# HGRN of a decoder trunk: log k moved into the exponent of the levels, and level scores summed by three wide additions

## The chip, the cores and the metric

One core of one Trainium2 chip runs the whole program. The metric is the device time of one execution in microseconds (us); lower is better. The kernel before has a median of 681.6 us over 3 runs.

## What is computed

Two residual layers over 512 tokens of width 1024. Each layer normalizes its input, projects it once, runs three mixers, gates them and projects back. The change lies in the second (odd) layer's HGRN mixer: 4 heads of width 64, chunked linear recurrence. With log decay `lf` per token and channel, `b` its running sum inside a chunk, and k = exp(lf - f) for the forget input f:

```
scores = einsum('bhtd,bhsd,bhtsd->bhts', qt, kt, exp(b_t - b_s))   # s <= t
intra  = einsum('bhts,bhse->bhte', scores, vt)
st     = st * exp(b_last) + einsum('bhsd,bhse->bhde', kt * exp(b_last - b), vt)
```

Every factor k appears beside an exponential of a difference of `b`.

## The kernel before, in words

Channels lie on the 128 partitions, the 512 tokens along the row. The 4 heads are worked as two pairs (`hgrn_pair`, called twice from line 1373), each with 128 channels and chunks of 128 tokens. The running sum `b` is one scan (L1147).

A chunk's triangle of scores is built by levels. `level(hh)` cuts the tokens into blocks of 2*hh, takes the last `b` of the first half as reference, and makes one tile `hx`: second half exp(b - ref) times q (L1162, L1164, L1167), first half exp(ref - b) times k (L1163, L1164, L1168). Matmuls of `hx` with itself then give that level's scores. Levels 64 and 32 go straight into the score tiles `hat` (L1179, L1192). Levels 16, 8, 4, 2 (`small`, L1209) and the last two (diagonal and neighbour, `last`, L1218, which uses k itself) are multiplied by masks into six planes of `htm` (L1200), one tile for each head of the pair. L1226 sums the six planes with one strided reduction for each head into `hsm`, and four copies put the result into the diagonal blocks of `hat` (L1228, recorded as L490 on ScalarE or L492 on VectorE). `hat` feeds the matmuls L1255.

For the carried state, `he` = exp(b_last - b) (L1230, L1231) times k (L1232) is transposed by TensorE (L1235) and multiplied with the values (L1245). L1267 to L1273 normalize and gate the output.

Around it stand the input projections of the layer (L235 under `pj`), with weights split into a rounded part `hi` on ScalarE (L226) and a rest `lo` on VectorE (L227). TensorE, VectorE and ScalarE each run their queue in order. The order itself is made when the program is built, by a list planner that takes ready instructions by priority and its own cost estimates. Four bands set the priorities: the straight text (HGRN among it) counts from 0, evacuations of projections from 50, weight splits from 500000, head norms from 600000, projections from 1000000. So projections fill what HGRN leaves on TensorE, and any changed duration can sort the queues anew.

Of the kernel before, what the change touches and what calls it, by code (L numbers as in the profile page):

```python
# [13 lines left out]
AF = mybir.ActivationFunctionType  # L14
OP = mybir.AluOpType
AX = mybir.AxisListType
PSUM = bass.MemoryType.PSUM

P = 128
D = 1024  # L20
S = 512
NM = 256
NT = S // P
# [123 lines left out]
def tile_trunk(ctx, tc, x_in, memT_in, w_mem, e_w_in, e_w_out, o_w_in, o_w_out, ln_g, w2_in, a2_in,  # L147
               prm_in, cst_in, out):
    nc = tc.nc
    V, A, G, T = nc.vector, nc.scalar, nc.gpsimd, nc.tensor  # L150
# [6 lines left out]
    def tl(pool, shape, name, dt=F32, **kw):  # L157
        return pool.tile(shape, dt, tag=name, name=name, **kw)
# [3 lines left out]
    def pj(name="pj"):  # L162
        if name == "t":
            tn[0] ^= 1
            name = f"t{tn[0]}"
        return ps.tile([P, 512], F32, tag=name, name=name, bufs=2 if name == "pj" else 1)
# [22 lines left out]
    def C(name, j=None):  # L189
        return cst[name] if j is None else cst[name][:, j:j + 1]  # L190
# [89 lines left out]
    def col(name, n=1):  # L280
        c = sum(w for _, w in cols.values())
        cols[name] = (c, n)
        return small[:, c:c + n]
# [203 lines left out]
    def evac(dst, src, kind="d"):  # L487
        evac_n[kind] += 1
        if EVP[kind][evac_n[kind] % len(EVP[kind])] == "A":
            A.activation(dst, src, AF.Copy)  # L490
        else:
            V.tensor_copy(dst, src)  # L492
# [169 lines left out]
    with ExitStack() as ph:  # L662
# [10 lines left out]
        for h in range(2):  # L673
            t = pj("t")
# [46 lines left out]
    for n, sgn in (("aq", -0.125), ("ak", 1.0), ("cq", -0.125), ("ck", 1.0)):  # L721
        g = col("g" + n)
        tmp = col("t" + n)
# [409 lines left out]
    def hgrn_pair(dp, q, qx, fd, idn, sgd, rm128):  # L1133
        qd = qx[:, 0]
        f3 = lambda t: t.rearrange("p (c t) -> p c t", t=P)
        e = tl(dp, [P, S], "he")
        lf = tl(dp, [P, S], "hlf")
# [2 lines left out]
        A.activation(e, e, AF.Exp, scale=-1.0)  # L1140
        A.activation(e, e, AF.Ln, bias=ones)
        V.tensor_tensor(lf, lf, e, op=OP.subtract)
        k = tl(dp, [P, S], "hk")
        V.tensor_tensor(k, lf, fd, op=OP.subtract)
        A.activation(k, k, AF.Exp)
        b = tl(dp, [P, S], "hb")
        V.tensor_tensor_scan(b, rm128, lf, 0.0, op0=OP.mult, op1=OP.add)  # L1147
        hs = [slice(0, 64), slice(64, 128)]
        q4 = [slice(32 * j, 32 * j + 32) for j in range(4)]
        at = [tl(dp, [P, NT, P], f"hat{p}", bufs=1) for p in range(2)]  # L1150
        for p in range(2):
            G.memset(at[p], 0.0)
        tmp = [tl(dp, [P, 6, NT, 32], f"htm{p}", bufs=1) for p in range(2)]
        hl = C("hlev").rearrange("p (l t) -> p l t", t=32)

        def level(hh):
            x = tl(dp, [P, S], "hx", bufs=3)
            bv = b.rearrange("p (c z h) -> p c z h", z=2, h=hh)
            xv = x.rearrange("p (c z h) -> p c z h", z=2, h=hh)
            nb = S // (2 * hh)  # L1160
            ref = bv[:, :, 0, hh - 1:hh].to_broadcast([P, nb, hh])
            V.tensor_tensor(xv[:, :, 1, :], bv[:, :, 1, :], ref, op=OP.subtract)  # L1162
            V.tensor_tensor(xv[:, :, 0, :], ref, bv[:, :, 0, :], op=OP.subtract)  # L1163
            A.activation(x, x, AF.Exp)  # L1164
            qv = qd.rearrange("p (c z h) -> p c z h", z=2, h=hh)
            kv = k.rearrange("p (c z h) -> p c z h", z=2, h=hh)
            V.tensor_tensor(xv[:, :, 1, :], xv[:, :, 1, :], qv[:, :, 1, :], op=OP.mult)  # L1167
            V.tensor_tensor(xv[:, :, 0, :], xv[:, :, 0, :], kv[:, :, 0, :], op=OP.mult)  # L1168
            return x

        def lev64():
            x = level(64)
            s = s2()
            for p in range(2):
                for i in range(NT):
                    T.matmul(s[0:64, p, i * 64:i * 64 + 64], x[hs[p], i * P:i * P + 64],
                             x[hs[p], i * P + 64:(i + 1) * P], start=True, stop=True)
            for p in range(2):
                A.activation(at[p][0:64, :, 64:128], s[0:64, p, 0:256].rearrange("p (i t) -> p i t", t=64), AF.Copy)  # L1179

        def lev32():
            x = level(32)
            s = s2()
            for p in range(2):
                for i in range(NT):
                    for m in range(2):
                        o = i * P + 64 * m
                        T.matmul(s[q4[2 * m], p, i * 32:i * 32 + 32], x[hs[p], o:o + 32], x[hs[p], o + 32:o + 64],
                                 start=True, stop=True)
            for p in range(2):  # L1190
                for m in range(2):
                    A.activation(at[p][q4[2 * m], :, 64 * m + 32:64 * m + 64],  # L1192
                                 s[q4[2 * m], p, 0:128].rearrange("p (i t) -> p i t", t=32), AF.Copy)
# [3 lines left out]

        def masked(s, g0):
            for p in range(2):
                V.tensor_tensor(tmp[p][:, g0:g0 + 2], s[:, p, 0:2 * P].rearrange("p (l i t) -> p l i t", l=2, t=32),  # L1200
                                hl[:, g0:g0 + 2, None, :].to_broadcast([P, 2, NT, 32]), op=OP.mult)

        def small(g0):
            s = s2()
            for l in range(2):
                x = level(16 >> (g0 + l))
                for p, i, j, o in blocks:
                    c = l * P + i * 32
                    T.matmul(s[q4[j], p, c:c + 32], x[hs[p], o], x[hs[p], o], start=True, stop=True)  # L1209
            masked(s, g0)  # L1210

        def last():
            s = s2()
            A.activation(qx[:, 1], lf, AF.Exp)
            V.tensor_tensor(qx[:, 1], qx[:, 1], qd, op=OP.mult)
            sv = s[:, :, 0:2 * P].rearrange("p a (l t) -> p a l t", t=P)
            for p, i, j, o in blocks:
                T.matmul(sv[q4[j], p, :, i * 32:i * 32 + 32], k[hs[p], o], qx[hs[p], :, o], start=True, stop=True)  # L1218
            masked(s, 4)

        todo = {"A": lev64, "B": lev32, "0": lambda: small(0), "2": lambda: small(2), "4": last}
        for c in HGO:
            todo[c]()
        for p in range(2):
            sm = tl(dp, [P, NT, 32], "hsm")
            V.tensor_reduce(sm, tmp[p].rearrange("p l i t -> p i t l"), axis=AX.X, op=OP.add)  # L1226
            for j in range(4):
                evac(at[p][q4[j], :, 32 * j:32 * j + 32], sm[q4[j]], "h")  # L1228
        e = tl(dp, [P, S], "he")
        V.tensor_tensor(f3(e), f3(b)[:, :, P - 1:P].to_broadcast([P, NT, P]), f3(b), op=OP.subtract)  # L1230
        A.activation(e, e, AF.Exp)  # L1231
        V.tensor_tensor(e, e, k, op=OP.mult)  # L1232
        t = pj("t")
        for i in range(NT):
            T.transpose(t[:, i * P:(i + 1) * P], e[:, i * P:(i + 1) * P], ident)  # L1235
# [34 lines left out]
        t = pj("t")  # L1270
# [61 lines left out]
    def odd_layer():  # L1332
# [6 lines left out]
        with ExitStack() as ph2:  # L1339
# [32 lines left out]
            for q in range(2):  # L1372
                hgrn_pair(dp, q, qd[q], fd[q], idn, sg[4 + q], rm128)
# [67 lines left out]
```

## Time and profile before

| what | value |
|---|---|
| median of 3 runs | 681.6 us (679.17, 681.6, 681.83) |
| profiled execution, its own time | 678.45 us |
| its span, first to last instruction | 676.2 us |
| mean granted TensorE clock | 0.997 |
| busy share: TensorE / VectorE / ScalarE | 96% / 73% / 49% |
| HGRN stage, from the first scan to the last `hat` matmul | 395 to 455 us of the span |

A busy share is an average over all stages. TensorE's busy time is modelled, so 96% busy does not say that it computes at its peak. The granted clock is given as a share of 2.4 GHz; 0.5 is the lower level, 1.2 GHz. "issue" as a releaser means that the engine waited for nothing that the profile shows.

### The profile page before, as it was taken

The page shows a single profiled execution, that of the slowest core. Times are in us where ns is not written, and L with a number is a line of the kernel's source. Part 1 is how long each engine was busy: PE and PEld are TensorE (multiplying, and loading weights), DVE is VectorE, ACT ScalarE, POOL GpSimd, SP SyncE. Part 2 cuts the span into 40 slices and gives each one's busy share as a digit, 9 for nine tenths or more (in the row PEclk, how much of TensorE's full clock was granted, in tenths as well). Part 3 has the DMA queues.
Part 4 walks back from the last instruction along what each step waited for, and adds up shares of the span by engine and source line. Part 5 has one row for each costly group of instructions (what it writes and reads, how often), then busy time and mean ns, then how long its engine had stood idle before and what let it go on. Part 6 is the DMA issues. An engine that isn't in the chain of part 4 may idle for free.

```text
span 676.2 us, 15423 instructions
## 1 busy us (share of the span) xinstructions
PE 651.4 (96%) x6192; PEld 551.8 (82%) x6192; DVE 491.7 (73%) x1394; ACT 328.2 (49%) x969; POOL 6.8 (1%) x21
## 2 busy tenths in 40 slices
PE   8999999999999998999999999999999999999997
PEld 5877777898888875567999987779999977577997
DVE  4996685888847978857747986985645658789853
ACT  5667346442222357545415585545355336478420
POOL 1000000000000000000000000000000000000000
PEclk9999999999999999999999999899999999999999
DMA  9471222322101340101524433014232331000323
GB/s 303 125 192 31 64 63 64 99 64 64 39 28 38 88 155 5 39 1 40 172 94 126 131 93 96 3 54 127 72 101 89 95 93 32 1 1 0 96 63 124
DMA packets 62905, 53.52 MB, mean 79 GB/s; under 512 B 3377, under 2 KB 61041, under 8 KB 62834
## 3 DMA queue, kind: packets, MB, share of 16 engines
q1 hardware_dynamic: 62834, 52.55, 25.7%
q8 instruction: 48, 0.79, 0.5%
q14 instruction: 23, 0.19, 0.1%
HBM read 50.44 MB, written 2.10 MB: 78 GB/s over the span
## 4 chain that ended last, share of the span: by engine, by line
PE 71%; DVE 17%; ACT 6%; DMA 3%; issue 2%; SPq 0%; ACTq 0%; DVEq 0%
PE pj L235 50%; PE s L466 3%; DMA raw<-in_e_w_in_dram 2%; DVE lo L227 1%; PE t L1306 1%; PE t L520 1%; PE t L572 1%; ACT pr L547 1%; PE s L882 1%; PE c L876 1%; PE t L512 1%; PE t L449 1%; PE t L842 1%; DVE pr L554 1%; ACT hi L226 1%
## 5 line engine op out<-in xcount | busy, mean ns | idle before, releaser
L226 ACT ACTIVATE hi<-raw 128x512 fp32r<-128x512 f32 (+2 forms) x164 | 89.9, 596 | 95.8 <-PE pj L235 75.8
L227 DVE TENSOR_TENSOR lo<-raw,hi 128x512 fp32r<-128x512 f32 (+2 forms) x164 | 101.7, 648 | 25.3 <-PE pj L235 21.9
L235 PE MATMUL pj<-hi,act_hi 128*128 128x256 f32 x672 | 104.2, 285 | 0.7 <-ACT act_hi L274 0.5
L235 PE MATMUL pj<-hi,act_lo 128*128 128x256 f32 x672 | 102.8, 284 | 0.0
L235 PE MATMUL pj<-lo,act_hi 128*128 128x256 f32 x672 | 102.2, 284 | 0.0
L235 PEld LDWEIGHTS pj<-hi,act_hi 128*128 128x128 f32 x672 | 89.7, 188 | 3.5 <-ACT act_hi L274 1.2
L235 PEld LDWEIGHTS pj<-hi,act_lo 128*128 128x128 f32 x672 | 89.2, 188 | 1.0 <-issue 0.5
L235 PEld LDWEIGHTS pj<-lo,act_hi 128*128 128x128 f32 x672 | 88.9, 188 | 0.8 <-issue 0.3
L235 PE MATMUL pj<-act_lo,hi 128*128 128x512 f32 (+1 forms) x248 | 71.0, 409 | 0.0
L235 PE MATMUL pj<-act_hi,lo 128*128 128x512 f32 (+1 forms) x248 | 69.5, 409 | 0.0
L235 PE MATMUL pj<-act_hi,hi 128*128 128x512 f32 (+1 forms) x248 | 67.7, 403 | 0.0
L235 PEld LDWEIGHTS pj<-act_hi,lo 128*128 128x128 f32 (+1 forms) x248 | 45.7, 190 | 11.2 <-issue 1.2
L235 PEld LDWEIGHTS pj<-act_hi,hi 128*128 128x128 f32 (+1 forms) x248 | 45.0, 187 | 10.6 <-issue 0.5
L235 PEld LDWEIGHTS pj<-act_lo,hi 128*128 128x128 f32 (+1 forms) x248 | 44.6, 187 | 10.7 <-issue 0.5
L586 DVE TENSOR_TENSOR x<-pj,x 128x256 f32<-128x256 f32 x64 | 27.0, 422 | 34.2 <-PE pj L235 34.0
L617 ACT ACTIVATE sq<-pj 128x64 f32<-128x64 f32 x144 | 30.0, 226 | 32.0 <-DVE nat L492 22.2
L478 ACT ACTIVATE pr<-pr,mx 128x128 f32<-128x128 f32 (+3 forms) x56 | 31.0, 557 | 2.6 <-DVE mx L476 2.2
L617 ACT ACTIVATION_READ_ACCUMULATOR sq<-pj 128x1 f32 x144 | 29.2, 211 | 0.0
L476 DVE CUSTOM_DVE_ANT_0 pr<-s,mask 128x128 f32<-128x128 f32 (+3 forms) x56 | 25.8, 483 | 3.8 <-PE t L512 1.8
L490 ACT ACTIVATE PT<-t 128x512 f32<-128x512 f32 (+3 forms) x28 | 13.9, 498 | 26.4 <-PE t L563 10.4
L429 ACT ACTIVATE th<-pj 128x512 f32<-128x512 f32 x16 | 9.5, 596 | 30.6 <-PE pj L235 30.6
L547 ACT ACTIVATE pr<-s,mmx 128x256 f32<-128x256 f32 x32 | 14.7, 482 | 7.4 <-DVE mmx L544 7.4
(408 smaller groups left out, 1049.7 us busy)
## 6 DMA issues: line engine op xcount, KB each, us to landing
raw<-in_o_w_in_dram SPq DMA_DIRECT2D x20, 512.0 KB, 3.6
raw<-in_e_w_in_dram SPq DMA_DIRECT2D x36, 256.0 KB, 3.4
raw<-in_e_w_in_dram SPq DMA_DIRECT2D x10, 512.0 KB, 4.1
x<-in_x_dram SPq DMA_DIRECT2D x8, 512.0 KB, 6.1
raw<-in_o_w_in_dram SPq DMA_DIRECT2D x16, 256.0 KB, 3.5
raw<-in_o_w_out_dram SPq DMA_DIRECT2D x8, 512.0 KB, 3.4
raw<-in_e_w_out_dram SPq DMA_DIRECT2D x4, 512.0 KB, 3.5
raw<-in_w_mem_dram SPq DMA_DIRECT2D x4, 512.0 KB, 3.5
```

The source lines that it names most:

```text
L226: A.activation(hi[:, z, :n], r, AF.Copy)
L227: V.tensor_tensor(lo[:, z, :n], r, hi[:, z, :n].bitcast(F32), op=OP.subtract)
L235: T.matmul(o, lh(k), rh(k), start=c == 0, stop=c == tot - 1)
L429: A.activation(th, o, AF.Tanh, scale=0.5)
L449: T.transpose(t[:, i * P:(i + 1) * P], nat[:, i, c0:c0 + P], ident)
L466: T.matmul(o, qT[a][h, qs], kT[b][h, ks], start=c == 0, stop=c == 2)
L476: V.tensor_tensor_reduce(pr[:, p, :n], s[:, p, :n], mask[0][:, 384 - i * P:512], 1.0, 1e38, op0=OP.add, op1=OP.min, accum_out=mx[:, p:p + 1])
L478: A.activation(pr[:, p, :n], pr[:, p, :n], AF.Exp, bias=mx[:, p:p + 1], scale=-1.0, accum_out=rs[:, p:p + 1])
L490: A.activation(dst, src, AF.Copy)
L547: A.activation(pv[:, p, ii, :], sv[:, p, ii, :], AF.Exp, bias=mx[:, c:c + 1], scale=-1.0, accum_out=rs[:, c:c + 1])
L586: V.tensor_tensor(x[i][:, cs], o, x[i][:, cs], op=OP.add)
L617: A.activation(sq[:, h0 + h], o[:, 64 * (h0 + h):64 * (h0 + h + 1)], AF.Square, accum_out=ss[:, i * nh + h:i * nh + h + 1])
```

## The change

`bk` = lf - f = log k is kept, and replaced by b - log k after the scan. The lower half of each level becomes exp(ref - bk), which holds k already, and so does exp(b_last - bk) for the state. The products L1168 and L1232 go; k itself stays for `last`. The two `htm` tiles become one, with both heads side by side; the two reductions L1226 become three additions over both heads, and the copies into `hat` read the first plane in place.

```
+        bk = tl(dp, [P, S], "hbk")
+        V.tensor_tensor(bk, lf, fd, op=OP.subtract)
         k = tl(dp, [P, S], "hk")
-        V.tensor_tensor(k, lf, fd, op=OP.subtract)
-        A.activation(k, k, AF.Exp)
+        A.activation(k, bk, AF.Exp)
         b = tl(dp, [P, S], "hb")
         V.tensor_tensor_scan(b, rm128, lf, 0.0, op0=OP.mult, op1=OP.add)
+        V.tensor_tensor(bk, b, bk, op=OP.subtract)
...
-        tmp = [tl(dp, [P, 6, NT, 32], f"htm{p}", bufs=1) for p in range(2)]
+        tmp = tl(dp, [P, 2, 6, NT * 32], "htm", bufs=1)
...
+            bkv = bk.rearrange("p (c z h) -> p c z h", z=2, h=hh)
...
-            V.tensor_tensor(xv[:, :, 0, :], ref, bv[:, :, 0, :], op=OP.subtract)
+            V.tensor_tensor(xv[:, :, 0, :], ref, bkv[:, :, 0, :], op=OP.subtract)
             A.activation(x, x, AF.Exp)
             qv = qd.rearrange("p (c z h) -> p c z h", z=2, h=hh)
-            kv = k.rearrange("p (c z h) -> p c z h", z=2, h=hh)
             V.tensor_tensor(xv[:, :, 1, :], xv[:, :, 1, :], qv[:, :, 1, :], op=OP.mult)
-            V.tensor_tensor(xv[:, :, 0, :], xv[:, :, 0, :], kv[:, :, 0, :], op=OP.mult)
...
+        V.tensor_tensor(tmp[:, :, 0:3], tmp[:, :, 0:3], tmp[:, :, 3:6], op=OP.add)
+        V.tensor_tensor(tmp[:, :, 0], tmp[:, :, 0], tmp[:, :, 1], op=OP.add)
+        V.tensor_tensor(tmp[:, :, 0], tmp[:, :, 0], tmp[:, :, 2], op=OP.add)
         for p in range(2):
-            sm = tl(dp, [P, NT, 32], "hsm")
-            V.tensor_reduce(sm, tmp[p].rearrange("p l i t -> p i t l"), axis=AX.X, op=OP.add)
+            sm = tmp[:, p, 0].rearrange("p (i t) -> p i t", t=32)
             for j in range(4):
                 evac(at[p][q4[j], :, 32 * j:32 * j + 32], sm[q4[j]], "h")
         e = tl(dp, [P, S], "he")
-        V.tensor_tensor(f3(e), f3(b)[:, :, P - 1:P].to_broadcast([P, NT, P]), f3(b), op=OP.subtract)
+        V.tensor_tensor(f3(e), f3(b)[:, :, P - 1:P].to_broadcast([P, NT, P]), f3(bk), op=OP.subtract)
         A.activation(e, e, AF.Exp)
-        V.tensor_tensor(e, e, k, op=OP.mult)
```

## Rows read from the trace of the kernel before

**Rows 1.** The page, part 1: engine, busy us, share of the span, instructions.
```profile
PE 651.4 (96%) x6192; PEld 551.8 (82%) x6192; DVE 491.7 (73%) x1394; ACT 328.2 (49%) x969; POOL 6.8 (1%) x21
```
**Rows 2.** Windows by stage: stretch, its length, busy time of PE, PEld, DVE, ACT, POOL, then PE's clock.
```profile
390.00:416.00 26.00, 25.05 (x166) 21.90 (x165) 17.68 (x37) 20.30 (x32) 0.00 (x0) 1.00 0.39 114
416.00:456.00 40.00, 35.76 (x862) 28.33 (x860) 36.47 (x92) 18.47 (x41) 0.99 (x2) 0.96 0.09 26
456.00:500.00 44.00, 44.00 (x369) 44.00 (x368) 23.42 (x83) 19.69 (x107) 0.00 (x0) 1.00 0.34 104
```
**Rows 3.** Waits of PE from 396 to 456 us: total us, times, longest us.
```profile
PE s L1209 <- issue: 1.8, 2, 0.9
PE s L1255 <- DVE hat L492: 1.0, 2, 0.7
PE s L1209 <- ACT hat L1192: 0.9, 1, 0.9
PE t L1235 <- DVE he L1232: 0.8, 1, 0.8
PE s L1188 <- DVE hx L1168: 0.5, 1, 0.5
```
**Rows 4.** Groups of VectorE instructions by line.
```profile
L1226 DVE TENSOR_REDUCE hsm<-htm 128x128 f32<-128x768 f32 x4 | 6.1, 1524 | 0.0
L1168 DVE TENSOR_TENSOR hx<-hx,hk 128x256 f32<-128x256 f32 x12 | 5.0, 418 | 0.6 <-ACT hx L1164 0.6
L872 DVE TENSOR_TENSOR R<-R,cmr 128x768 f32<-128x768 f32 x5 | 4.8, 950 | 0.0
```
**Rows 5.** Timeline of VectorE, from 393 us: start, duration, instruction.
```profile
393.77 0.69 DVE L1142 TENSOR_TENSOR hlf<-hlf,he 128x512 f32<-128x512 f32 x1 [0.86 <-ACT he L1141]
394.49 0.69 DVE L1144 TENSOR_TENSOR hk<-hlf,fd 128x512 f32<-128x512 f32 x1
395.10 1.22 DVE L1147 TENSOR_TENSOR_SCAN hb<-rm,hlf 128x512 f32<-128x512 f32 x1
...
396.82 0.42 DVE L1162 TENSOR_TENSOR hx<-hb 128x256 f32<-128x256 f32 x1
397.15 0.42 DVE L1163 TENSOR_TENSOR hx<-hb 128x256 f32<-128x256 f32 x1
...
402.40 0.68 DVE L1232 TENSOR_TENSOR he<-he,hk 128x512 f32<-128x512 f32 x1
```
**Rows 6.** Timeline of VectorE and TensorE at the end of the second pair.
```profile
446.60 1.54 DVE L1226 TENSOR_REDUCE hsm<-htm 128x128 f32<-128x768 f32 x1
...
448.05 0.69 DVE L1232 TENSOR_TENSOR he<-he,hk 128x512 f32<-128x512 f32 x1
...
450.45 1.52 DVE L1226 TENSOR_REDUCE hsm<-htm 128x128 f32<-128x768 f32 x1
...
453.31 1.75 PE L1255 MATMUL s<-idn,hat 128*128 128x64 f32 x14 [0.68 <-DVE hat L492]
```
**Rows 7.** Windows of 2 us before and in the fall of TensorE's clock, columns as in rows 2.
```profile
420.00:422.00 2.00, 1.51 (x98) 1.19 (x96) 2.00 (x6) 1.04 (x4) 0.00 (x0) 1.00 0.00 0
422.00:424.00 2.00, 0.81 (x62) 0.54 (x51) 1.97 (x5) 1.63 (x7) 0.00 (x0) 1.00 0.03 8
424.00:426.00 2.00, 1.37 (x20) 0.89 (x19) 2.00 (x6) 0.62 (x1) 0.00 (x0) 1.00 0.00 0
426.00:428.00 2.00, 2.00 (x68) 1.72 (x68) 1.80 (x6) 1.35 (x3) 0.00 (x0) 0.51 0.03 8
428.00:430.00 2.00, 2.00 (x7) 1.63 (x6) 1.97 (x5) 1.47 (x3) 0.00 (x0) 0.64 0.00 0
```
**Rows 8.** Timeline of TensorE: eight projection matmuls at full and at half clock.
```profile
387.40 2.04 PE L235 MATMUL pj<-act_hi,lo 128*128 128x512 f32 x8
...
427.56 2.89 PE L235 MATMUL pj<-act_hi,lo 128*128 128x512 f32 x8
```
**Rows 9.** Timeline of ScalarE around the exponential of k, first and second pair.
```profile
394.95 1.28 ACT L1214 ACT_TABLE_LOAD   x1
396.24 0.63 ACT L1214 ACTIVATE qd<-hlf 128x512 f32<-128x512 f32 x1
396.78 0.61 ACT L1145 ACTIVATE hk<-hk 128x512 f32<-128x512 f32 x1
...
426.30 0.63 ACT L1145 ACTIVATE hk<-hk 128x512 f32<-128x512 f32 x1 [1.68 <-DVE hk L1144]
```

More of the change, by code (lines that the diff above doesn't have):

```diff
@@ L1199, in masked @@
             for p in range(2):
-                V.tensor_tensor(tmp[p][:, g0:g0 + 2], s[:, p, 0:2 * P].rearrange("p (l i t) -> p l i t", l=2, t=32),
+                V.tensor_tensor(tmp[:, p, g0:g0 + 2].rearrange("p l (i t) -> p l i t", t=32), s[:, p, 0:2 * P].rearrange("p (l i t) -> p l i t", l=2, t=32),
                                 hl[:, g0:g0 + 2, None, :].to_broadcast([P, 2, NT, 32]), op=OP.mult)
```

## The prediction

> **What bounds the kernel now.** I read the busy shares first. TensorE is busy 96% of the span and VectorE 73% [rows 1], so over the whole program TensorE is the bound, and work taken off VectorE pays only where TensorE stands still for it. I therefore went to the windows by stage. The change touches 395 to 455 us. There the reader should see two things [rows 2]: from 416 to 456 us VectorE is busy 36.47 of 40 us, and TensorE, for once, only 35.76. Right behind it, from 456 to 500 us, TensorE is busy every microsecond. So the HGRN stage is VectorE's, what follows is TensorE's, and its work there needs nothing more of HGRN at once. The most that a faster HGRN can give is the time in which TensorE stands still inside the stage, plus what its clock loses there.
>
> Third, the waits of TensorE in the stage. They add to 1.8 + 1.0 + 0.9 + 0.8 + 0.5 = 5.0 us [rows 3]. Three of the five lines end on VectorE work that the change touches: L1235 waits for the product with k (L1232), L1188 for the product with k of a level (L1168), L1255 for the copies behind the reductions (L1226). Two do not: 1.8 us are "issue", in which no engine is waited for, and 0.9 us end on ScalarE's copies of level 32.
>
> Fourth, the clock. From 426 to 430 us TensorE's granted clock is 0.51 and then 0.64 of full [rows 7]: most of that stretch is at the lower level, 1.2 GHz. In the 6 us before, TensorE was busy only 1.51 + 0.81 + 1.37 = 3.69 us. Eight projection matmuls take 2.89 us there and 2.04 us elsewhere [rows 8].
>
> **The change, part by part, on VectorE.** A short operation's price is the distance to the next start where the queue is full: 397.15 - 396.82 = 0.33 us for 128x256 [rows 5], though one lasts 0.42 us [rows 4].
> - Products with k in the levels: six in each pair, 12 in all [rows 4], 12 x 0.33 = 4.0 us less.
> - The product for the state, L1232: two of 0.68 us less [rows 5, 6]. The new subtraction b - log k has the same shape: two more at the same price. Together nothing in sum, but a move: the cost leaves the stretch between ScalarE's exponential and the transposes, and goes to the front of the pair, behind the scan.
> - The reductions: four, each 448.05 - 446.60 = 1.45 us to the next start [rows 6], 5.8 us less.
> - The additions: in each pair one over 2 x 3 x 128 = 768 elements and two over 256. A 128x768 TENSOR_TENSOR lasts 0.95 us and a 128x256 one 0.42 [rows 4]. Each needs the one before, so whole durations count, with the gap of 394.49 - 393.77 - 0.69 = 0.03 us that L1144 shows behind L1142 [rows 5]: 0.95 + 0.42 + 0.42 + 2 x 0.03 = 1.85 us in a pair, 3.7 us in both. If other work goes into the gaps, the short ones cost 0.33, and it is 3.2.
>
> Sum on VectorE: 4.0 + 5.8 - 3.7 = 6.1 us less, of a stage in which it is nearly full.
>
> The reduction's row deserves a second look: 1.52 us for 768 elements, where a two-input addition of 768 takes 0.95 [rows 4]. The Trainium skill, page "VectorE: DVE Perf Modes", gives `tensor_reduce` in its section on the perf-mode tier table one element per cycle, the same rate as an fp32 `tensor_tensor`, and its section on the errata gives (N + 151)/0.96 ns for the latter; if the reduction went by that as well, two would cost about 1.9 us, an estimate from that page, and the additions would save nothing. The rows here differ by 0.57 us per reduction, and the sum goes by the rows.
>
> **What of it reaches TensorE.**
> - L1235 waits 0.8 us [rows 3]. L1232, which ends 402.40 + 0.68 = 403.08 us [rows 5], is the last thing before it. With the product gone, the transposes are ready when ScalarE's exponential ends. I take 0.8.
> - L1188 waits 0.5 us for L1168 of its level. That is one VectorE step of 0.33 us; the exponential and the product with q stay. I take 0.3.
> - L1255 waits twice, 1.0 us together. In the second pair the reductions run at 446.60 and 450.45, with other work between, and L1255 starts at 453.31 [rows 6]. The second reduction has to wait until `hsm`, a single buffer, is copied out. With the additions both heads' sums are ready 1.85 us after the masks, and no copy holds VectorE's sums back. I take 1.0. Late next would be the copies themselves, which stay eight in each pair.
> - "issue", 1.8 us, and ScalarE's 0.9 us: I take nothing. The number of small matmuls is unchanged, and so is ScalarE's work. Ends: 0 and 2.7.
> - The clock: between 426 and 430 us at most 2 x 0.49 + 2 x 0.36 = 1.7 us are lost [rows 7]. The fall follows a stretch with 2.3 us of idle time in 6, of which the list above removes 0.3 for certain and leaves "issue" and ScalarE's. So the fall may stay (0), go (1.7), or come later. Neither end is nearer by any row; I take half, 0.85.
>
> Sum: 0.8 + 0.3 + 1.0 + 0.85 = 2.95, say 3.0 us. Against the profiled execution, whose span of 676.2 us has 2.25 us around it, this makes 678.45 - 3.0 = 675.4. That execution was 3.15 us under the median of the runs; the three runs themselves lie 2.7 us apart. Taken off the median, the forecast is 681.6 - 3.0 = **678.6 us**. About 0.5%, 3.4 us, is what a measurement of this kernel can tell from no change, so the forecast stands just inside that bound.
>
> **The added wait.** The new subtraction overwrites log k, which ScalarE's exponential of k must have read. VectorE's queue is in order, so all behind it wait too: all six first-half subtractions of the pair. In the first pair L1144 ended at 395.18 us, and k's exponential came only at 396.78, behind a table load of 1.28 us and another exponential [rows 9]; it ended at 397.39. The scan and the second-half subtractions, which read b alone, cover this: the first L1163 ran at 397.15 [rows 5]. In the second pair ScalarE had stood idle for 1.68 us and took k's exponential at once [rows 9]. I cost the wait at nothing; without that cover it is 397.39 - 395.10 - 1.22 = 1.1 us in the first pair, at most 2.2 from L1144's end.
>
> **Rivals.**
> 1. *Nothing much arrives* (chance 0.25). The DVE queue shortens, but the planner sorts everything behind 395 us anew, and the small matmuls stop instead at what the change leaves: "issue", ScalarE's copies, the eight copies into `hat`. For it: 2.7 of the 5.0 us already end there. Against it: VectorE is 91% busy in the stage. Only L1235's 0.8 us come: 680.8 us.
> 2. *All VectorE waits and the clock's fall go* (0.17). For it: 6.1 us of VectorE work leave, more than the 5.0 us of waits. Against it: the fall follows partly from waits that stay. 5.0 - 1.8 + 1.7 = 4.9 us: 676.7 us.
> 3. *Slower: the added wait stops VectorE in the second pair* (0.13). Place: the subtraction b - log k of the second pair, in the full stretch from 416 us on, before any of the pair's first-half subtractions. If the new order puts a table load and other exponentials ahead of k's, as in the first pair, VectorE stands 2.2 us with nothing to cover it, TensorE's small matmuls wait as long, and the clock falls once more, 1.7 us. 2.2 + 1.7 - 2.1 (the three waits gained) = 1.8 us slower: 683.4. It decides from the point where k's exponential ends more than 2.1 us behind the scan. Against it: ScalarE is busy only 18.47 of 40 us there [rows 2].
>
> That the change does not do what it says I hold for nothing: k is needed by `last` alone, and no other reader is left.
>
> **How the numbers follow.** The forecast's own case (0.45) runs from 2.1 us gained with the clock's fall unchanged to 3.8 without it: 677.8 to 679.5. With a spread of the runs of about 1.2 us to each side, some 0.35 of it falls below 678.2, the bound of 0.5%. Of rival 2 nearly all does, of rival 1 little, so faster is 0.45 x 0.35 + 0.17 x 0.9 + 0.03 = 0.34. Slower by over 3.4 us needs rival 3 with a bad run, or a second such wait: half of 0.13, and a little for the new order elsewhere, 0.08. The rest, 0.58, is the same. The range takes in rival 2 with the spread below it and rival 3 above: 675.2 to 683.3.
>
> **What would show it.** In the changed profile VectorE's busy total should fall by about 7 us (durations, which overlap, count more than distances), the wait L1235 on VectorE should be gone, L1255 should not wait for copies over 0.3 us, and the stretch from the first scan to the last L1255 should shrink by 3 to 6 us. Wrong it would be if VectorE idles behind k's exponential, if the clock falls to 0.5 in more windows than two of 2 us, or if the waits return under "issue".

## The result, and the profile after

The changed kernel takes 683.59 us (median of 20 runs) against 679.54 us for the kernel before (20 runs beside them): ratio 1.0055, 95% interval 1.0042 to 1.0067. It is 4.05 us slower, where 3.0 us faster was forecast; 683.59 lies just outside the range. The 679.54 us are 2.1 us less than the median of three runs off which the forecast was taken: from this base the same terms give 676.5 us, and the miss is 7.1 us. Ratios, here and below, leave out runs in the slower state, which is one run only (before_spread, 689.43 us); medians and mean clocks are over all runs.

VectorE did what the sum said. The page of the profile, part 1, of the changed kernel:

```profile
PE 654.6 (96%) x6192; PEld 554.9 (81%) x6192; DVE 485.4 (71%) x1384; ACT 328.2 (48%) x969; POOL 6.8 (1%) x21
```

VectorE's busy time fell from 491.7 us [rows 1] to 485.4, that is 6.3 us. TensorE has the same 6192 matmuls and is busy 3.2 us longer. The stage windows, columns as in [rows 2], say where:

```profile
390.00:416.00 26.00, 24.61 (x162) 21.38 (x161) 17.32 (x39) 21.12 (x33) 0.00 (x0) 1.00 0.32 93
416.00:456.00 40.00, 34.93 (x839) 28.10 (x838) 31.52 (x84) 16.84 (x38) 0.99 (x2) 0.87 0.16 48
456.00:500.00 44.00, 44.00 (x357) 43.37 (x356) 23.00 (x82) 19.28 (x95) 0.00 (x0) 1.00 0.26 82
```

From 416 to 456 us VectorE is now busy 31.52 of 40 us instead of 36.47 [rows 2], less than TensorE's 34.93, and so it is no longer the fuller of the two. But TensorE is not busier, and its clock in the stage went from 0.96 to 0.87. The stage's length can be taken from the same projection matmuls at its two ends, first in the kernel before, then in the changed one (timeline of TensorE, then the window between the two starts, columns as in [rows 2]):

```profile
383.66 2.03 PE L235 MATMUL pj<-act_hi,hi 128*128 128x512 f32 x8
...
455.65 1.11 PE L235 MATMUL pj<-hi,act_hi 128*128 128x256 f32 x8
383.66:455.65 71.99, 66.80 (x1051) 54.98 (x1050) 59.83 (x145) 41.17 (x77) 2.29 (x6) 0.98 0.24 70
```
```profile
385.20 2.03 PE L235 MATMUL pj<-act_hi,hi 128*128 128x512 f32 x8
...
460.91 1.12 PE L235 MATMUL pj<-hi,act_hi 128*128 128x256 f32 x8
385.20:460.91 75.71, 69.26 (x1050) 57.66 (x1049) 53.32 (x135) 41.38 (x79) 2.28 (x6) 0.93 0.24 73
```

72.0 us became 75.7. Of the 5.3 us by which the spans of the two profiled executions differ, 3.7 lie in this stage, and 1.5 are the later start, ahead of the change (1.1 of them are idle time of TensorE in the first 40 us). In the stage TensorE is busy 2.5 us longer, 69.26 against 66.80, with the same matmuls, and idle 1.3 us longer, 6.45 against 5.19. The longer busy time goes with a lower clock, 0.93 instead of 0.98 in these windows. The windows of 2 us of the changed kernel, to be read against [rows 7]:

```profile
424.00:426.00 2.00, 1.01 (x79) 0.74 (x66) 1.97 (x4) 1.94 (x7) 0.00 (x0) 1.00 0.03 8
426.00:428.00 2.00, 1.09 (x16) 0.93 (x16) 2.00 (x6) 0.89 (x2) 0.00 (x0) 0.66 0.00 0
428.00:430.00 2.00, 2.00 (x65) 1.25 (x66) 0.87 (x3) 0.63 (x1) 0.00 (x0) 0.50 0.04 12
430.00:432.00 2.00, 2.00 (x24) 1.64 (x15) 1.68 (x4) 0.10 (x1) 0.00 (x0) 0.50 0.00 0
432.00:434.00 2.00, 2.00 (x7) 1.54 (x6) 1.62 (x5) 2.00 (x4) 0.00 (x0) 0.63 0.00 0
...
448.00:450.00 2.00, 0.41 (x49) 0.32 (x38) 1.22 (x3) 0.00 (x0) 0.00 (x0) 1.00 0.80 250
450.00:452.00 2.00, 1.94 (x10) 1.54 (x10) 1.61 (x3) 0.00 (x0) 0.00 (x0) 0.64 0.80 238
452.00:454.00 2.00, 2.00 (x7) 1.55 (x6) 1.77 (x7) 0.59 (x2) 0.00 (x0) 0.51 0.09 30
```

The first fall is twice as long, at most 2 x (0.34 + 0.50 + 0.50 + 0.37) = 3.4 us lost instead of 1.7, and there is a second one, at most 2 x (0.36 + 0.49) = 1.7 us, behind a stretch in which TensorE was busy 0.41 of 2 us. How much of this is the change's doing two traces can't tell: all runs but one of the kernel before have mean clocks from 0.994 to 0.997, that is 4.1 to 2.0 us lost of a span of 677.5 us, and its profiled execution (0.997) is one of those that lost least. The idle time is to be seen in TensorE's waits, 390 to 460 us, to be read against [rows 3]:

```profile
PE s L1210 <- issue: 2.8, 2, 1.6
PE t L1237 <- ACT he L1234: 1.0, 1, 1.0
PE s L1210 <- ACT hat L1193: 0.8, 1, 0.8
PE t L1274 <- DVE hO L1271: 0.7, 1, 0.7
PE s L1189 <- DVE hx L1169: 0.6, 1, 0.6
```

They are not shorter but longer, 5.9 us where the five lines of before make 5.0. The wait behind the reductions is gone; "issue" grew from 1.8 to 2.8 us; the transposes (L1237) wait 1.0 us for the exponential, where they waited 0.8 for the product; a wait for the normalized output (L1274) is new.

I looked for the cause of both in the order of instructions on TensorE. Second pair, before and after (x: matmuls of the levels, k: those of `last`, H: L1255 or L1257, Q: L1259 or L1261, t: transposes, P: projections; counts as in the program, while the trace records each x, k, H and Q twice):

```
before  Q6 x32 P3 x8 P3 x16 k32 P1 x32 P3 t4 P1 x32 P4 P8 P1 t4 H1 P7 P5 H7
after   Q6 x57 x8 t4 P7 P1 x16 k21 t4 k11 x64 P7 P8 P3 H1 P1 H7
```

Before, no more than 48 small matmuls (96 records) stand between two projections here. After, x16 k21 t4 k11 x64 do: 232 in the count that the expectations below use (twice each, the four transposes with them). HGRN has the higher priority; I read the new order so that with shorter VectorE work the planner counts its matmuls as ready sooner and puts them in one row. That is theory 1: the order, not the operations, costs the time, through longer stalls and falls of the clock. Theory 2: the operations cost it, the added wait or the dependent additions.

The first pair fits this picture less well, which the expectations below leave out. Its order, from the same timelines:

```
before  P6 x64 x8 P5 x16 k32 x32 P4 x32 P14 H1
after   P6 x64 x8 P3 x16 k32 x32 P4 x32 P20 H1
```

Its long row, x16 k32 x32, is the same before and after, and the first fall follows this row in both kernels.

### The profile page after: what moved, and what is told of

It is laid out like the page before. It is cut to its first block, busy times and chain, and to the rows that moved or that the text cites. A ratio compares the mean times of both kernels' runs of the same rounds, so it can differ in the third digit from the quotient of the medians.

```text
span 681.5 us, 15404 instructions
## 1 busy us (share of the span) xinstructions
PE 654.6 (96%) x6192; PEld 554.9 (81%) x6192; DVE 485.4 (71%) x1384; ACT 328.2 (48%) x969; POOL 6.8 (1%) x21
## 4 chain that ended last, share of the span: by engine, by line
PE 72%; DVE 16%; ACT 6%; DMA 3%; issue 2%; SPq 0%; DVEq 0%; ACTq 0%
PE pj L235 51%; PE s L466 2%; DVE lo L227 1%; PE t L1308 1%; PE t L520 1%; PE t L572 1%; ACT pr L547 1%; DMA raw<-in_e_w_in_dram 1%; PE c L876 1%; PE s L882 1%; PE t L512 1%; PE t L449 1%; DVE act_lo L425 1%; DMA memT<-in_memT_dram 1%; PE t L842 1%
```

## The experiments

| run | ratio to before | 95% interval | median us | mean clock |
|---|---|---|---|---|
| kernel before (67 runs beside the experiments) | 1 | | 678.76 to 679.73 | 0.9956 |
| changed kernel | 1.0055 | 1.0042 to 1.0067 | 683.59 | 0.9919 |
| fold_only | 1.0060 | 1.0038 to 1.0081 | 682.04 | 0.9927 |
| adds_only | 1.0017 | 1.0003 to 1.0031 | 680.23 | 0.9954 |
| after_fill2nd | 1.0046 | 1.0028 to 1.0063 | 682.09 | 0.9953 |
| after_fill | 0.9985 | 0.9972 to 0.9997 | 677.91 | 0.9996 |
| before_spread | 1.0084 | 1.0054 to 1.0114 | 685.74 | 0.9893 |
| after_spread | 0.9959 | 0.9947 to 0.9971 | 677.29 | 0.9994 |
| after_spread_again | 0.9957 | 0.9940 to 0.9973 | 676.93 | 1.0000 |
| adds_spread | 0.9991 | 0.9963 to 1.0019 | 679.04 | 0.9938 |
| after_spread1st | 0.9977 | 0.9963 to 0.9991 | 677.76 | 0.9976 |
| after_nowait | 1.0051 | 1.0033 to 1.0069 | 683.17 | 0.9917 |
| after_spread_nowait | 0.9964 | 0.9950 to 0.9979 | 677.62 | 0.9997 |
| after_ballast | 1.0083 | 1.0057 to 1.0108 | 684.66 | 0.9990 |

The mean clock is the mean of the granted clocks of a kernel's timed runs.

**Each half alone.** fold_only keeps the reductions, adds_only keeps the products with k. Against the changed kernel, in excerpts:

```
fold_only
...
-        V.tensor_tensor(tmp[:, :, 0:3], tmp[:, :, 0:3], tmp[:, :, 3:6], op=OP.add)
...
+            V.tensor_reduce(sm, tmp[p].rearrange("p l i t -> p i t l"), axis=AX.X, op=OP.add)
...
adds_only
...
-            V.tensor_tensor(xv[:, :, 0, :], ref, bkv[:, :, 0, :], op=OP.subtract)
+            V.tensor_tensor(xv[:, :, 0, :], ref, bv[:, :, 0, :], op=OP.subtract)
...
+            V.tensor_tensor(xv[:, :, 0, :], xv[:, :, 0, :], kv[:, :, 0, :], op=OP.mult)
...
+        V.tensor_tensor(e, e, k, op=OP.mult)
```

> Log k in the exponent, but the two reductions as before. TensorE's order in the second pair has the same unbroken run of 232 small matmuls between two groups of projections as the changed kernel (before: 96 at most). Theory 1 (order: the planner takes the projections out from between the small matmuls, the clock falls in the second pair too): as slow as the changed kernel, ratio to before 1.004 to 1.007, and the clock at 0.5 around 450 us. Theory 2 (the operations themselves cost it: the added wait on the exponential of k, or the additions in a row): about 1.005 if it is the wait, 1.000 or less if it is the additions.

> The three additions, but the products with k as before. The longest runs of small matmuls in the second pair are 172 and 176. Theory 1: between the two, ratio 1.000 to 1.004, with the second fall of the clock shorter or gone. Theory 2: 1.005 if the additions are the cause, 0.996 to 0.999 if it is the wait, since then a gain of 1 to 2 us on VectorE is all that is left.

fold_only, log k in the exponent without the additions, brings the whole loss, 1.0060, with the row of 232 in its second pair and a mean clock of 0.9927. The additions alone cost 0.17%. Both came as theory 1 had it, but the result of fold_only fits the added wait of theory 2 as well.

**The wait taken away.** The subtraction gets a tile of its own, so VectorE does not wait for the exponential of k:

```
+        lk, bk = bk, tl(dp, [P, S], "hbl")
-        V.tensor_tensor(bk, b, bk, op=OP.subtract)
+        V.tensor_tensor(bk, b, lk, op=OP.subtract)
```

> The changed kernel with b - log k in a tile of its own, so that its subtraction does not wait for the exponential of k; the planner's order else, again with a run of 232 small matmuls in the second pair. Theory 1 (order and clock): the wait was 0.5 us in the first pair and none in the second, so it stays slow, 1.004 to 1.006. Theory 2 in the form of the slower rival of the prediction (the added wait is the cause): 1.000 or less.

In the changed kernel the wait is there once, in the first pair (timeline of VectorE):

```profile
398.85 0.69 DVE L1149 TENSOR_TENSOR hbk<-hb,hbk 128x512 f32<-128x512 f32 x1 [0.52 <-ACT hk L1146]
```

Without it the time stays at 1.0051 and the clock at 0.9917. The wait is not the cause. Two of the 12 runs of after_nowait had a clock of 0.996 and 0.997 and took 679.46 and 679.84 us, as long as the kernel before; the ten others (0.989 to 0.994) took 682.6 to 685.9.

**The same operations in another order.** Only the priorities of the levels' matmuls are changed: `late` gives a group the priority of a chosen projection matmul, so that it cannot run ahead of it. The fill versions give a group the very priority of that projection matmul; the spread versions, shown here in excerpts, widen the steps between the projections' priorities to 4 and put the group between two of them.

```
+        def late(key, fn):
+            keep = tc.cur_priority
+            if key in FILL[q]:
+                tc.cur_priority = base + 4 * FILL[q][key] - 2
+            fn()
+            tc.cur_priority = keep
...
-                    T.matmul(s[q4[j], p, c:c + 32], x[hs[p], o], x[hs[p], o], start=True, stop=True)
+                    late(g0 + l, lambda: T.matmul(s[q4[j], p, c:c + 32], x[hs[p], o], x[hs[p], o], start=True, stop=True))
...
+    FILL = ({'A': 9, 'B': 12, '4': 15, 0: 18, 1: 22}, {3: 18, 'A': 20, 'B': 23, '4': 26, 0: 29, 1: 33})
```

> The changed kernel, every operation of it; only the priorities of the second pair's small matmuls differ, so that three or four projection matmuls stand between its levels (longest run 70 from level 64 on, 164 ahead of it). Theory 1: the second fall of the clock (about 1.7 us lost) and the 1.6 us issue stall behind 448 us go; ratio to before 0.999 to 1.002. Theory 2: the operations are the same, so it stays at 1.004 to 1.007.

> As the run before, with the first pair's levels spread between projections as well (longest run there 128, then 62; 172 at the start of the second pair). Theory 1: the first fall of the clock (3.4 us lost in the changed kernel, 1.7 before) shrinks or goes as well; ratio 0.994 to 0.999. Theory 2: 1.004 or more, as nothing is taken from the operations and the small matmuls start later.

With the second pair filled, its fall went, but the time only to 1.0046, outside the 0.999 to 1.002 that theory 1 had: a miss. Its mean clock, 0.9953, is about that of the kernel before, 0.9956, and yet it is about 3 us slower. So the second pair's row and its fall are not the main part of the loss. The first pair's fall remained, 4 x (0.32 + 0.50 + 0.03) = 3.4 us at most in this trace, as in that of the changed kernel. Windows of 4 us of after_fill2nd:

```profile
424.00:428.00 4.00, 1.86 (x81) 1.45 (x71) 3.97 (x9) 2.74 (x8) 0.00 (x0) 0.68 0.01 4
428.00:432.00 4.00, 4.00 (x72) 2.85 (x71) 2.28 (x7) 0.63 (x1) 0.00 (x0) 0.50 0.02 6
432.00:436.00 4.00, 4.00 (x18) 3.00 (x16) 2.82 (x10) 3.84 (x8) 0.00 (x0) 0.97 0.00 0
...
448.00:452.00 4.00, 4.00 (x136) 2.78 (x128) 2.17 (x5) 0.60 (x1) 0.00 (x0) 1.00 0.72 205
452.00:456.00 4.00, 3.27 (x73) 2.66 (x73) 2.14 (x4) 0.00 (x0) 0.00 (x0) 1.00 0.19 62
```

With both pairs filled the changed kernel is slightly faster than before, 0.9985, and 10 of its 11 runs have a clock of 0.999 or 1.000. Not one operation differs from the kernel at 1.0055. This run speaks against theory 2: the operations do not cost the time in every order. It does not show that the change's new row of 232 is the price, for the 4.2 us between after_fill2nd and after_fill come from the first pair, whose long row the kernel before has too.

> The changed kernel in the same spread order (longest run 128, then 92 once, else 64 to 72). Theory 1: clock 1.00 in both pairs, and with the clock out of the way the operations show their worth: ratio 0.993 to 0.998, level with the kernel before in the spread order or up to 2 us under it. Theory 2: 2 us or more above the kernel before in the spread order.

> The changed kernel in the spread order a second time, beside the variant without the wait. Theory 1: 0.994 to 0.998 and a clock of 0.999 to 1.000 in nearly every execution. Theory 2: 1.000 or more.

> The spread order and no wait of the subtraction on the exponential of k. Theory 1: the wait is worth at most its 0.5 us, so level with the spread run or 0.5 to 1 us under it, 0.993 to 0.997. Theory 2 (the wait is the cause): 2 us or more under it.

> The changed kernel with only its first pair spread; the second pair keeps a run of 172 and one of 232. Theory 1: the first fall of the clock goes, the second near 450 us stays with its issue stall: ratio 1.000 to 1.003, that is half way from the changed kernel (1.0055) to the kernel with both pairs spread (0.9985). Theory 2: 1.0055.

The spread order gave 0.9959, and 0.9957 when repeated: the best version of the study, 2.4 to 2.6 us under the kernel before. Taking the wait away as well changed nothing (0.9964). Spreading the first pair alone did better than expected, 0.9977: its second pair still has a row of 232, but in the profiled execution its issue stall was 0.7 us instead of 1.6 and the clock held, and six of the 12 runs had a clock of 0.999 or 1.000. The row ends at 447 us:

```profile
440.00:444.00 4.00, 3.44 (x120) 2.60 (x119) 4.00 (x18) 3.12 (x9) 0.00 (x0) 1.00 0.03 7
444.00:448.00 4.00, 3.04 (x136) 2.48 (x125) 2.84 (x8) 0.88 (x2) 0.00 (x0) 1.00 0.20 46
```

So a long row does not by itself bring the clock down. And the two pairs are not worth the same: with the first pair spread the changed kernel is 5.8 us faster (683.59 to 677.76), and spreading the second as well takes off another 0.5 (677.29).

**The kernel before in the spread order** was the widest miss of the study:

> The kernel before, with every operation of it; only the priorities differ, so that in both pairs two to four projection matmuls stand between the levels' small matmuls (longest run 128 at the first level, 64 to 72 after). Theory 1 (order: long runs of small matmuls and the waits in them let the clock fall): before's own fall at 426 us (1.7 us) and its issue stalls (1.8 us) go, ratio 0.995 to 0.998, clock 1.00. Theory 2 (the changed operations cost the time): nothing here is changed, so 1.000, or above it as the small matmuls start later.

It came out at 1.0084 with a mean clock of 0.9893. Its profiled execution was the one of seven with a clock of 0.999 and took 678.18 us, so no trace shows the falls of the others; TensorE's waits in it, 388 to 465 us:

```profile
PE s L1269 <- DVE hat L496: 2.8, 3, 1.2
PE t L1249 <- DVE he L1246: 0.9, 1, 0.9
PE s L1222 <- issue: 0.3, 1, 0.3
```

The waits under "issue" are down to 0.3 us, but L1269 (L1255 of the kernel before) now waits 2.8 us for the copies behind the reductions, where it waited 1.0 [rows 3]. after_spread has no such wait. That it is what brings the clock down in the other six runs is not shown. So the spread order pays with the changed operations and not with the old ones; whether the fill order, or the first pair spread alone, would help the kernel before was not run. The additions alone in the spread order:

> The additions alone, without log k in the exponent, in the spread order (first pair as in the two others; in the second 164 in a run at its start, then 72 and 128). Theory 1: clock 1.00 or one short fall, ratio 0.994 to 0.999. Theory 2: 1.000 or more.

Of its 12 runs, six had a clock of 0.999 or 1.000 and took 675.0 to 676.4 us, five one of 0.984 to 0.987 and took 681.7 to 684.0, and one (0.997) took 682.1. The profiled execution is one of those with the low clock; windows of 4 us:

```profile
428.00:432.00 4.00, 3.43 (x15) 2.44 (x13) 4.00 (x12) 1.85 (x5) 0.00 (x0) 1.00 0.00 0
432.00:436.00 4.00, 3.26 (x46) 3.01 (x50) 3.12 (x11) 0.90 (x3) 0.89 (x2) 0.99 0.01 4
436.00:440.00 4.00, 4.00 (x126) 2.89 (x126) 3.92 (x13) 2.30 (x4) 0.10 (x1) 0.50 0.02 4
440.00:444.00 4.00, 4.00 (x50) 3.04 (x52) 3.39 (x13) 1.18 (x3) 0.00 (x0) 0.50 0.00 0
444.00:448.00 4.00, 4.00 (x80) 2.78 (x75) 0.69 (x1) 2.28 (x7) 0.00 (x0) 0.50 0.42 135
448.00:452.00 4.00, 4.00 (x26) 2.60 (x21) 3.30 (x8) 0.00 (x0) 0.00 (x0) 0.50 0.00 0
452.00:456.00 4.00, 4.00 (x139) 3.50 (x140) 2.33 (x5) 0.84 (x2) 0.00 (x0) 0.88 0.44 135
```

TensorE stood idle for 1.3 us of 8, and the clock fell and stayed at the lower level for 16 us, in which small groups and projections alternated. So theory 1 has to be put more loosely than I had it: each fall shown here came behind idle time among small matmuls, in a long row's issue stall or, as here, in an order that spreads them. That the idle time is the cause is argued, not shown, and a spread order does not keep the clock up by itself.

**Work added between.** Six 128x256 matmuls that feed nothing stand in the middle of each level of the small kind and of `last`, 60 in all:

```
+        def ballast(s, p):
+            for _ in range(6):
+                T.matmul(s[:, p, 256:512], act_hi[:, 0, 0:P], act_hi[:, 1, 0:256], start=True, stop=True)
...
                 for p, i, j, o in blocks:
+                    if (p, i, j) == (1, 0, 0):
+                        ballast(s, l)
```

> The changed kernel with 60 added 128x256 matmuls (six in the middle of each level of the small kind and of the last levels, on unused columns), which feed nothing: 60 x 0.12 = 7.2 us more work for TensorE, between the small matmuls. Theory 1: the clock stays at 1.00, or falls once where it fell twice, so that the added work costs less than itself: 2 to 5 us over the changed kernel, 1.008 to 1.013 to before. If the falls come from the idle time alone and not from what runs between, the clock stays as in the changed kernel (0.992) and the time is 7 us or more over it, 1.016.

684.66 us: the added work, 60 x 0.12 = 7.2 us (an estimate from the timelines, where eight 128x256 matmuls start 0.96 us before the next eight), cost 1.1 us over the changed kernel, and three of four runs had a clock of 1.000. Windows of 4 us:

```profile
424.00:428.00 4.00, 3.17 (x140) 2.73 (x138) 4.00 (x9) 2.54 (x6) 0.00 (x0) 1.00 0.01 4
428.00:432.00 4.00, 4.00 (x59) 3.18 (x52) 4.00 (x10) 2.43 (x5) 0.00 (x0) 1.00 0.01 4
...
444.00:448.00 4.00, 3.71 (x139) 3.01 (x138) 3.90 (x11) 2.53 (x8) 0.00 (x0) 1.00 0.02 4
448.00:452.00 4.00, 4.00 (x120) 3.45 (x114) 1.75 (x6) 0.00 (x0) 0.00 (x0) 1.00 0.43 135
```

It does not separate idle time from the kind of work: the added matmuls also took the place of idle time ("issue" is 0.8 us in this run, not 2.8).

## Why the prediction was wrong

**VectorE's sum** was right: 6.1 us by distances, about 7 in busy time; 6.3 were measured. The additions take 0.96, 0.42 and 0.43 us with gaps of 0.03 and 0.04 in the second pair, as costed (timeline of VectorE):

```profile
451.15 0.96 DVE L1225 TENSOR_TENSOR htm<-htm 128x768 f32<-128x768 f32 x1
452.14 0.42 DVE L1226 TENSOR_TENSOR htm<-htm 128x256 f32<-128x256 f32 x1
452.60 0.43 DVE L1227 TENSOR_TENSOR htm<-htm 128x256 f32<-128x256 f32 x1
```

That VectorE was the fuller engine of the stage, and would stop being so, was right too.

**The three waits, 2.1 us gained**, came to 0.7 net. L1255's 1.0 us went, as argued. L1235's 0.8 us became 1.0 of L1237 on ScalarE, and L1188's 0.5 us became 0.6. The step "with the product gone, the transposes are ready when ScalarE's exponential ends" was true: before, the product ended 8.0 us behind the start of the scan, at 403.08 us [rows 5]; now the exponential ends 6.9 us behind it. The scan and the exponential of the changed kernel:

```profile
396.53 1.22 DVE L1148 TENSOR_TENSOR_SCAN hb<-rm,hlf 128x512 f32<-128x512 f32 x1
...
402.85 0.62 ACT L1234 ACTIVATE he<-he 128x512 f32<-128x512 f32 x1
```

But the new order moved the transposes forward as well. They stand behind 44 of the 128x256 projection matmuls instead of 55, that is about 11 x 0.12 = 1.3 us sooner, and so TensorE waits for them again. The matmuls of L1188 stand behind three of the projection matmuls before them instead of five.

**The step that failed is the clock, together with "issue, 1.8 us: I take nothing".** I took half of a fall as a gain, 0.85 us, and bounded the term between 0 and 1.7 us gained; a loss was not in the bounds. Measured, the clock lost more: in the profiled stage TensorE was busy 2.5 us longer with the same matmuls, and over the runs the time lost at the lower level grew from (1 - 0.9956) x 677.5 = 3.0 us to (1 - 0.9919) x 681.6 = 5.5 us, that is by 2.5 us at most, since part of that time was idle. "issue" was not 0 to the good but 1.0 us to the bad, and the idle time of the stage grew by 1.3 us, where the sum had taken 2.1 us from it. Behind both is one omission. The text said that any changed duration can sort the queues anew, and then summed gains on the old queues. That another order takes the loss away is shown (after_fill, after_spread). What in the changed kernel brings the loss stays open: most of what another order gives back lies in the first pair, whose long row did not change, and how much of it is clock and how much is stalls no run separates.

Of the signs named beforehand, the right ones came on VectorE and in the waits L1235 and L1255, but the stretch from the first scan to the last L1255 did not shrink by 3 to 6 us; it grew from 60.0 to 61.7. Two signs of being wrong came: three windows of 2 us at 0.50 or 0.51, and 2.8 us under "issue".

**The rivals.** The slower one had the right sign and a part of the mechanism: it let the clock fall once more, for 1.7 us, and the profile has a second fall of at most 1.7 us. But it hung the fall on the added wait, and after_nowait shows that the wait has no part in it; that its 683.4 us lies beside the measured 683.59 is luck, as it stood for a loss of 1.8 us, from a median 2.1 us too high, and 4.05 were lost. Rival 1 named "issue" and ScalarE's copies as what would stop the small matmuls; it did not see that "issue" would grow. Rival 2, with the clock's fall gone, is what after_spread shows in kind, under another order; its 676.7 us is near 677.3 and 676.9 by luck too, for it stood for 4.9 us gained and 2.4 to 2.6 were. The chance of 0.08 for slower by over 0.5% was too small for a change whose main price, a new order, had no bound in the sum.

**The Trainium skill on the reduction** (page "VectorE: DVE Perf Modes", section on the perf-mode tier table): it gives `tensor_reduce` the same rate as an fp32 `tensor_tensor`. The rows do not agree for this one, 1.52 us for a reduction of 768 elements [rows 4] against 0.96 us for the addition of 768 elements, and the sum was right to go by the rows. In time adds_only does not decide it, since its order changed as well.

## What to carry to other kernels

Where a planner orders the queues, price a change on the queues that it will make: look at where the new order puts the instructions that wait, and what TensorE waits for among its small matmuls, before you count VectorE's savings. When a change takes load off one engine and nothing is gained, read the granted clock of the stage next to its waits. And try the same operations under other priorities before you drop the change: here that turned 0.55% slower into 0.4% faster. Try them on the old kernel too, since the order that helped the changed kernel made the kernel before 0.84% slower.

## What was not expected of the hardware

The clock fell to its lower level although TensorE never stood still in the stage for over 1.0 us at a time in the kernel before (1.6 in the changed one). Before the falls it was busy 3.69 of 6 us [rows 7] and, in adds_spread, 6.69 of 8 us. after_spread kept 1.00 through 3.67 + 3.10 of 8 us, and so idle time alone does not tell:

```profile
424.00:428.00 4.00, 3.67 (x136) 2.73 (x135) 3.87 (x8) 3.06 (x9) 0.00 (x0) 1.00 0.02 4
428.00:432.00 4.00, 3.10 (x77) 2.26 (x76) 3.97 (x11) 3.98 (x8) 0.00 (x0) 1.00 0.01 2
```

How long the clock is down differs from run to run with one and the same program: by its mean clock adds_spread kept it up in six of 12 runs, and the five with 0.984 to 0.987 took about 6 us longer. What exactly decides it, and what the engine waits for under "issue" in a long row of small matmuls, stays open; no run here separates them.
